# A gated delta rule with two groups of products per chunk, one pass for the weighted keys, and a weight pool at another address

## The chip, the cores and the metric

The kernel runs on one core of one Trainium2 chip. The metric is device time in microseconds (us), the median of several executions; lower is better. PE is the matrix engine (its weight load is listed as PEld), DVE the vector engine, ACT the scalar engine, POOL the GpSimd engine, SP the engine that issues most of the DMAs. Each engine runs its instructions in the order in which they stand in its queue.

## The reference

One decoder layer for 1024 prompt tokens and 8 requests of 4 new tokens each (1056 columns in all), model width 1024, float32:

```
p   = rmsnorm(x) @ w_in          # split: q,k,v of attention | conv input | z | a,b | gate_A | gate_B
o_A = stick-breaking attention   # 8 heads of 64, causal, no softmax
o_B = gated delta rule           # 4 heads, a 128x128 state each
m   = sigmoid(gate_A)*(o_A @ w_pa) + sigmoid(gate_B)*(o_B @ w_pb);   x = x + m @ w_o
x   = x + relu(rmsnorm(x) @ w_up)**2 @ w_down;   y = rmsnorm(x)
```

The part that the change touches is the delta rule, evaluated in chunks of tokens. For each chunk, with the state s of the head, U and W from a triangular solve, and decay factors in the operands:

```
v_new = U-part - W @ s
o     = (q * decay) @ s + (q @ k.T * decay) @ v_new
s     = s * exp(g_last) + (k * decay).T @ v_new
```

## The kernel before

**Number format.** A dense product in float32 is made of three products in the reduced format fp32r: a high part of the weights by a high part of the input (line 140), high weights by low input (141), low weights by high input (142). They are called stream matmuls here: 128x128 weights, and 256, 272 or 288 columns that move past them. The columns are cut into four pieces (`CX`: 256, 256, 256, 288) in the first half of the program and into two halves further on. All other products (of the delta rule, the transposes by `tr`) are plain float32; a 128x128 one stands as "x2" in the profile, that is as two instructions.

**Order.** The whole program is written in Python, but a planner that runs when the program is built decides in which order each engine's queue takes the instructions, from costs of its own; `tc.issue_after` and `tc.high_priority` steer it. In the first half, the dense products (`pd_uq`, `pd_uk`, `pd_uv`: conv inputs of a head; `pd_z`; `pd_aq`, `pd_ak`, `pd_av`: attention's q, k, v; `pd_g`: the gates) fill the queue of PE, and the short products of the delta rule stand between them in small runs. Later parts: attention among the gates' products (from about 600 us), the merge (`pb`, `pa`), output projection (`px`), up projection (`pu`), down projection (`pw`, then `pv`).

**The delta rule.** `gdn_head(h)` is called for the four heads. It solves the triangular systems of all eight chunks of 128 tokens together (U and nw, the negative of W), where line 544 weights the keys of one chunk into the tile kb (two buffers) and line 545 multiplies it by U. Then a loop over the chunks c carries the state st:

- product y (PSUM tile p6): `U.vb` (line 554) plus `nw.st` (line 556);
- DVE scales it into y2 (line 558), ACT copies it into yv (line 560);
- product s (p8): `kn.y2` (line 562), which DVE adds to the decayed state: the next st (line 565);
- product o (p7): `AT.yv` (line 569) plus `qe.st` (line 571), which ACT copies out (572) and squares (573).

p6, p7 and p8 all come from one pool `psg` of two PSUM banks, so the third tile waits for the first to be read. In the profile's names AT is `E`, qe is `cgb`, st is `st`, kn is `kn`. In the order listings a name such as `y0_5` is the tile y of head 0, chunk 5.

**Addresses.** Tiles lie in SBUF one behind the other, pool behind pool. The staging tiles and the two buffers each of `wh` and `wl` in `wpool` hold the weights of `pd_aq`, `pd_ak`, `pd_av`, `pd_g`, of `pb` and `pa`, and of the first pair of conv inputs. The other weights lie in the pools `gw` (further conv inputs, z) and, later, in pools of their own. In the built program, the byte address of a weight tile within a partition, taken modulo 256, and that of the moving columns are:

| product | weights, before | weights, after | moving columns, before | after |
|---|---|---|---|---|
| pd_aq, pd_ak, pd_av, pd_g, first conv pair | 192 | 64 | 0 | 0 |
| pb | 192 | 64 | 128 | 0 |
| pa | 192 | 64 | 0 to 192 | 0 to 192 |
| pd_uk, pd_uq, pd_uv (the rest), pd_z | 64 | 64 | 0 | 0 |
| pu, px | 64 | 64 | 0, second half 128 in places | the same |
| pw | 192 | 192 | 128 | 128 |

The conv job, the z job and the pools further on are laid out so that sizes below them decide their addresses: `z_job` has a tile of T + 48 words, of which T are used.

Of the kernel before, what the change touches and what calls it, by code (L numbers as in the profile page):

```python
# [18 lines left out]
P = 128  # L19
# [19 lines left out]
def hybrid_step(ctx, tc, x_prompt, x_sample, cache_k, cache_v, page_table, state_conv, state_ssm,  # L39
# [13 lines left out]
    cst = pool("cst")  # L53
    wctx = ExitStack()
    wpool = pool("wpool", 2, stack=wctx)
    kctx = ExitStack()
    keep = pool("keep", stack=kctx)
    dr = ctx.enter_context(tc.tile_pool(name="dr", bufs=1, space=DRAM))
# [13 lines left out]
    def gtile(name):  # L72
        return psg.tile([P, 512], F32, tag="g", name=name)
# [30 lines left out]
            w0s.append(st)  # L104
    ident = cst.tile([P, P], F32, name="ident")
    make_identity(nc, ident)
    ones = cst.tile([P, P], F32, name="ones")
    V.memset(ones, 1.0)
    powc = cst.tile([P, 2], F32, name="powc")
# [256 lines left out]
        return (1536 + i * P, f"u{name}", evac), cv  # L366

    def z_job(h):
        z = zp.tile([P, T + 48], F32, tag="zz", name=f"z{h}")[:, 0:T]

        def evac(c, o, n, pt):
            S_.activation(z[:, o:o + n], pt[:, :n], AF.Copy)
            if c == 3:
                S_.activation(z, z, AF.Silu)
                G.tensor_copy(zs[:, h, :], z[:, NP:T])
                SY.dma_start(z_d[h], z[:, 0:NP])

        return 3072 + h * P, f"z{h}", evac
# [10 lines left out]
    def c8(ap):  # L389
        return ap.rearrange("p (c f) -> p c f", f=P)  # L390

    def gdn_head(h):
# [145 lines left out]
        for hf in range(2):  # L538
            hs = slice(hf * 512, (hf + 1) * 512)
            p5 = gtile(f"wt{h}_{hf}")  # L540
            for i in range(4):
                c = hf * 4 + i
                kb = gk.tile([P, P], F32, tag="kb", name=f"kb{h}_{c}", bufs=2)
                V.tensor_scalar(kb, kn[:, cs_[c]], s3[:, c:c + 1], None, op0=ALU.mult)
                PE.matmul(p5[:, i * P:(i + 1) * P], lhsT=kb, rhs=U[:, cs_[c]], start=True, stop=True)
            S_.activation(nw[:, hs], p5, AF.Copy, scale=-1.0)

        on = nw
# [2 lines left out]
        for c in range(NC):  # L551
            sl = slice(c * P, (c + 1) * P)
            p6 = gtile(f"y{h}_{c}")
            PE.matmul(p6[:, 0:P], lhsT=U[:, sl], rhs=vb[:, sl], start=True, stop=(c == 0))
            if c > 0:
                PE.matmul(p6[:, 0:P], lhsT=nw[:, sl], rhs=st, start=False, stop=True)
            y2 = gk.tile([P, P], F32, tag="y2", name=f"y2{h}_{c}", bufs=2)
            V.tensor_scalar(y2, p6[:, 0:P], egc[:, c, h:h + 1], None, op0=ALU.mult)
            yv = gk.tile([P, P], F32, tag="yv", name=f"yv{h}_{c}", bufs=2)
            S_.activation(yv, p6[:, 0:P], AF.Copy)  # L560
            p8 = gtile(f"s{h}_{c}")
            PE.matmul(p8[:, 0:P], lhsT=kn[:, sl], rhs=y2, start=True, stop=True)
            sn = gk.tile([P, P], F32, tag="st", name=f"st{h}_{c}", bufs=2)
            if c > 0:
                V.scalar_tensor_tensor(sn, st, egl[:, c, h:h + 1], p8[:, 0:P], op0=ALU.mult, op1=ALU.add)
            else:
                V.tensor_copy(sn, p8[:, 0:P])
            p7 = gtile(f"o{h}_{c}")
            PE.matmul(p7[:, 0:P], lhsT=AT[:, sl], rhs=yv, start=True, stop=(c == 0))
            if c > 0:  # L570
                PE.matmul(p7[:, 0:P], lhsT=qe[:, sl], rhs=st, start=False, stop=True)
            S_.activation(on[:, sl], p7[:, 0:P], AF.Copy)
            S_.activation(jk_, p7[:, 0:P], AF.Square, accum_out=f_[:, c:c + 1])
            st = sn
# [560 lines left out]
    tbs = [tbp.tile([P, T], F32, name=f"tb{j}") for j in range(KT)]  # L1135
    obctx = ExitStack()
    obp = pool("obp", stack=obctx)
    obh, obl = [None] * 4, [None] * 4

    def ob_tiles(c):  # L1140
# [586 lines left out]
```

## Time and profile before

| | |
|---|---|
| median of three runs | 1692.62 us (1691.89 to 1697.1) |
| profiled execution | 1702.95 us, span 1701.2 us, granted clock 0.994 |
| PE busy in the span | 1656.6 us (97%), 14046 instructions |
| DVE, ACT, POOL busy | 1174.4 us (69%), 778.3 us (46%), 229.7 us (14%) |

The profiled execution took 10.33 us (0.6%) longer than the median of the runs; its span is 1.75 us shorter than its own time. The rows of the groups of instructions give a line of the kernel, an engine, an operation, what it writes and reads, the tile sizes, how many there were, their busy time and the mean duration of one, and the idle time of that engine just before them. A matmul's duration in them (some 280 ns) runs from its start to its end in a pipeline, so the next one starts well before: what PE's time is made of is the distance from start to start, which the timeline shows (columns: start in us, duration in us, engine, line, operation).

### The profile page before, as it was taken

Reading aid. Unit: us, or ns where it says so; the run is one execution under the profiler, and the core shown is the slowest. Engines: PE = TensorE matmul, PEld = TensorE weight load, DVE = VectorE, ACT = ScalarE, POOL = GpSimd, SP = SyncE. Lnnn points to the kernel's source line nnn. Section 1 sums busy time; section 2 is a strip of 40 time slices with the busy share of each in tenths; the row PEclk is TensorE's granted clock in tenths of the full one; section 3 lists DMA queues with packets and bytes.
Section 4 is the critical chain, followed back from the end, with each engine's and each line's share of the span. In section 5 each row is a group of like instructions: output and inputs, shape, how many; then the busy total and the mean of one; then the engine's idle time right before and its main releaser. Section 6 shows DMA issues by size and latency. Waiting matters only on the chain.

```text
span 1701.2 us, 34901 instructions
## 1 busy us (share of the span) xinstructions
PE 1656.6 (97%) x14046; PEld 1603.9 (94%) x14046; DVE 1174.4 (69%) x2363; ACT 778.3 (46%) x1556; POOL 229.7 (14%) x249
## 2 busy tenths in 40 slices
PE   7999999999999999999999999999999999999998
PEld 6999999999998789988999999999999999999998
DVE  6666676877334327889776488887777688688964
ACT  5453434343424225555533356554445563444455
POOL 2120111110004226665300000000000000000000
PEclk9999999999999999999999999999999999999999
DMA  5142233235537567996144645455443665442232
GB/s 182 38 119 81 69 95 106 86 112 147 153 99 216 156 176 168 217 239 190 26 146 131 177 134 146 148 149 172 152 150 115 233 224 208 158 159 97 96 113 78
DMA packets 260207, 240.88 MB, mean 142 GB/s; under 512 B 55907, under 2 KB 217796, under 8 KB 260045
## 3 DMA queue, kind: packets, MB, share of 16 engines
q1 hardware_dynamic: 255094, 227.90, 44.6%
q0 software_dynamic: 3200, 10.52, 2.1%
q8 instruction: 110, 1.80, 0.5%
q10 hardware_dynamic: 1750, 0.23, 0.1%
q14 instruction: 53, 0.43, 0.1%
HBM read 164.02 MB, written 74.58 MB: 140 GB/s over the span
## 4 chain that ended last, share of the span: by engine, by line
PE 86%; DVE 7%; DMA 4%; issue 2%; ACT 1%; SPq 0%; DVEq 0%; POOLq 0%; ACTq 0%
PE pu L142 6%; PE pu L141 6%; PE pu L140 6%; PE pw L142 5%; PE pw L140 5%; PE pw L141 5%; PE pd_g L140 4%; PE pd_g L142 4%; PE pd_g L141 4%; PE wt L114 2%; PE po L1009 1%; PE px L141 1%; PE px L140 1%; PE px L142 1%; PE pa L141 1%
## 5 line engine op out<-in xcount | busy, mean ns | idle before, releaser
L141 PE MATMUL pu<-Xl,uh 128*128 128x272 f32 (+1 forms) x812 | 230.4, 284 | 0.0
L142 PE MATMUL pu<-Xh,ul 128*128 128x272 f32 (+1 forms) x812 | 229.3, 284 | 0.5 <-DVE ul L1272 0.5
L140 PE MATMUL pu<-Xh,uh 128*128 128x272 f32 (+1 forms) x812 | 229.5, 283 | 0.0
L140 PE MATMUL pw<-hc,w 128*128 128x272 f32 (+1 forms) x784 | 219.4, 284 | 2.4 <-ACT w L1536 2.4
L141 PE MATMUL pw<-hc,w 128*128 128x272 f32 (+1 forms) x784 | 219.4, 284 | 0.0
L142 PE MATMUL pw<-hc,w 128*128 128x272 f32 (+1 forms) x784 | 212.6, 284 | 1.5 <-DVE w L1537 1.5
L142 PEld LDWEIGHTS pu<-Xh,ul 128*128 128x128 f32 x812 | 152.8, 189 | 0.7 <-DVE ul L1272 0.7
L140 PEld LDWEIGHTS pu<-Xh,uh 128*128 128x128 f32 x812 | 152.8, 188 | 0.1
L141 PEld LDWEIGHTS pu<-Xl,uh 128*128 128x128 f32 x812 | 152.7, 188 | 0.0
L140 PEld LDWEIGHTS pw<-hc,w 128*128 128x128 f32 x784 | 148.1, 189 | 2.8 <-ACT w L1536 2.6
L140 PE MATMUL pd_g<-xh,wh_g 128*128 128x256 f32 (+1 forms) x512 | 149.7, 292 | 1.1 <-issue 1.1
L142 PE MATMUL pd_g<-xh,wl_g 128*128 128x256 f32 (+1 forms) x512 | 148.9, 291 | 1.2 <-issue 1.2
L141 PE MATMUL pd_g<-xl,wh_g 128*128 128x256 f32 (+1 forms) x512 | 149.2, 291 | 0.0
L141 PEld LDWEIGHTS pw<-hc,w 128*128 128x128 f32 x784 | 147.2, 188 | 0.0
L142 PEld LDWEIGHTS pw<-hc,w 128*128 128x128 f32 x784 | 144.3, 189 | 1.9 <-DVE w L1537 1.9
L140 PEld LDWEIGHTS pd_g<-xh,wh_g 128*128 128x128 f32 x512 | 97.7, 191 | 4.8 <-issue 4.3
L971 DVE TENSOR_TENSOR_SCAN pr<-am 128x127 f32<-128x127 f32 (+7 forms) x64 | 89.8, 1404 | 15.5 <-POOL am L967 11.7
L141 PEld LDWEIGHTS pd_g<-xl,wh_g 128*128 128x128 f32 x512 | 97.7, 191 | 2.9 <-issue 2.6
L142 PEld LDWEIGHTS pd_g<-xh,wl_g 128*128 128x128 f32 x512 | 97.6, 191 | 2.9 <-issue 2.7
L1536 ACT ACTIVATE w<-a 128x512 fp32r<-128x512 f32 x84 | 46.7, 620 | 97.3 <-PE pw L142 87.3
L1509 ACT ACTIVATE hc<-hc 128x528 fp32r<-128x528 f32 x98 | 62.0, 643 | 28.9 <-DMA hc<-hc_d 27.2
L967 POOL TENSOR_SCALAR am<-s 128x128 f32<-128x128 f32 (+7 forms) x64 | 71.8, 1122 | 11.0 <-DVE pr L971 5.8
(588 smaller groups left out, 5058.1 us busy)
## 6 DMA issues: line engine op xcount, KB each, us to landing
hc<-hc_d SPq DMA_DIRECT2D x94, 264.0 KB
hc_d<-t SPq DMA_DIRECT2D x14, 952.0 KB
a<-in_w_down_dram SPq DMA_DIRECT2D x52, 256.0 KB
hc_d<-t SPq DMA_DIRECT2D x13, 896.0 KB
ws_c<-in_w_in_dram SPq DMA_DIRECT2D x16, 512.0 KB
ws_wo<-in_w_o_dram SPq DMA_DIRECT2D x32, 256.0 KB
ua<-in_w_up_dram SPq DMA_DIRECT2D x16, 512.0 KB
ub<-in_w_up_dram SPq DMA_DIRECT2D x16, 512.0 KB
```

The source lines that it names most:

```text
L114: return PE.transpose(out, in_, ident[:k, :k])
L140: PE.matmul(pt[:, :n], lhsT=wh[k], rhs=xh[k], start=(k == 0), stop=False)
L141: PE.matmul(pt[:, :n], lhsT=wh[k], rhs=xl[k], start=False, stop=False)
L142: PE.matmul(pt[:, :n], lhsT=wl[k], rhs=xh[k], start=False, stop=(k == nk - 1))
L967: G.tensor_scalar(am[:, :n], s[:, :n], -1.0, 1.0, op0=ALU.mult, op1=ALU.add)
L971: V.tensor_tensor_scan(pr[:, n - 1:0:-1], am_r, am_r, 1.0, op0=ALU.mult, op1=ALU.bypass)
L1009: PE.matmul(po[64 * r:64 * r + 64, 0:P], lhsT=vn[:, b, rs], rhs=wts[hh, 2 * m + r][:, b * P:(b + 1) * P], start=(b == 0), stop=(b == 2 * m ...
L1509: S_.activation(tl[:, 0], tl[:, 1].bitcast(F32), AF.Copy)
L1536: S_.activation(tl[:, 0], src, AF.Copy)
```

## The change

Three things are done.

1. In `gdn_head`, the tile of o is taken before y2, and `qe.st` follows right behind `nw.st`; `AT.yv` then follows when yv is there, and `kn.y2` is put right behind `AT.yv`. Per chunk there are two groups of float32 products on PE instead of three.
2. The weighted keys of four chunks are made by one DVE instruction (128x512, a multiplication by a broadcast) into a tile `x2` with one buffer, where there were four (128x128) into `kb` with two buffers.
3. A tile `wpad` of 32 words stands first in `wpool`, and the z tile is shorter by 32 words: `wpool`'s weights move by 128 bytes, and what lies behind both stays. A tile `obpad` of 32 words stands first in `obp`, before the tiles obh and obl that move past the weights of `pb`.

```diff
--- before.py
+++ after.py
@@ -53,6 +53,7 @@
     cst = pool("cst")
     wctx = ExitStack()
     wpool = pool("wpool", 2, stack=wctx)
+    wpad = wpool.tile([P, 32], F32, name="wpad", bufs=1)
     kctx = ExitStack()
     keep = pool("keep", stack=kctx)
     dr = ctx.enter_context(tc.tile_pool(name="dr", bufs=1, space=DRAM))
@@ -104,6 +105,7 @@
             w0s.append(st)
     ident = cst.tile([P, P], F32, name="ident")
     make_identity(nc, ident)
+    V.memset(wpad, 0.0)
     ones = cst.tile([P, P], F32, name="ones")
     V.memset(ones, 1.0)
     powc = cst.tile([P, 2], F32, name="powc")
@@ -366,7 +368,7 @@
         return (1536 + i * P, f"u{name}", evac), cv
 
     def z_job(h):
-        z = zp.tile([P, T + 48], F32, tag="zz", name=f"z{h}")[:, 0:T]
+        z = zp.tile([P, T + 16], F32, tag="zz", name=f"z{h}")[:, 0:T]
 
         def evac(c, o, n, pt):
             S_.activation(z[:, o:o + n], pt[:, :n], AF.Copy)
@@ -538,11 +540,10 @@
         for hf in range(2):
             hs = slice(hf * 512, (hf + 1) * 512)
             p5 = gtile(f"wt{h}_{hf}")
+            kb = gk.tile([P, 4, P], F32, tag="x2", name=f"kb{h}_{hf}")
+            V.tensor_tensor(kb, c8(kn[:, hs]), s3[:, hf * 4:hf * 4 + 4].unsqueeze(2).to_broadcast([P, 4, P]), op=ALU.mult)
             for i in range(4):
-                c = hf * 4 + i
-                kb = gk.tile([P, P], F32, tag="kb", name=f"kb{h}_{c}", bufs=2)
-                V.tensor_scalar(kb, kn[:, cs_[c]], s3[:, c:c + 1], None, op0=ALU.mult)
-                PE.matmul(p5[:, i * P:(i + 1) * P], lhsT=kb, rhs=U[:, cs_[c]], start=True, stop=True)
+                PE.matmul(p5[:, i * P:(i + 1) * P], lhsT=kb[:, i], rhs=U[:, cs_[hf * 4 + i]], start=True, stop=True)
             S_.activation(nw[:, hs], p5, AF.Copy, scale=-1.0)
 
         on = nw
@@ -552,23 +553,24 @@
             sl = slice(c * P, (c + 1) * P)
             p6 = gtile(f"y{h}_{c}")
             PE.matmul(p6[:, 0:P], lhsT=U[:, sl], rhs=vb[:, sl], start=True, stop=(c == 0))
+            p7 = gtile(f"o{h}_{c}")
             if c > 0:
-                PE.matmul(p6[:, 0:P], lhsT=nw[:, sl], rhs=st, start=False, stop=True)
+                mark = PE.matmul(p6[:, 0:P], lhsT=nw[:, sl], rhs=st, start=False, stop=True)
+                with tc.issue_after(mark.ins):
+                    PE.matmul(p7[:, 0:P], lhsT=qe[:, sl], rhs=st, start=True, stop=False)
             y2 = gk.tile([P, P], F32, tag="y2", name=f"y2{h}_{c}", bufs=2)
             V.tensor_scalar(y2, p6[:, 0:P], egc[:, c, h:h + 1], None, op0=ALU.mult)
             yv = gk.tile([P, P], F32, tag="yv", name=f"yv{h}_{c}", bufs=2)
             S_.activation(yv, p6[:, 0:P], AF.Copy)
+            mark = PE.matmul(p7[:, 0:P], lhsT=AT[:, sl], rhs=yv, start=(c == 0), stop=True)
             p8 = gtile(f"s{h}_{c}")
-            PE.matmul(p8[:, 0:P], lhsT=kn[:, sl], rhs=y2, start=True, stop=True)
+            with tc.issue_after(mark.ins):
+                PE.matmul(p8[:, 0:P], lhsT=kn[:, sl], rhs=y2, start=True, stop=True)
             sn = gk.tile([P, P], F32, tag="st", name=f"st{h}_{c}", bufs=2)
             if c > 0:
                 V.scalar_tensor_tensor(sn, st, egl[:, c, h:h + 1], p8[:, 0:P], op0=ALU.mult, op1=ALU.add)
             else:
                 V.tensor_copy(sn, p8[:, 0:P])
-            p7 = gtile(f"o{h}_{c}")
-            PE.matmul(p7[:, 0:P], lhsT=AT[:, sl], rhs=yv, start=True, stop=(c == 0))
-            if c > 0:
-                PE.matmul(p7[:, 0:P], lhsT=qe[:, sl], rhs=st, start=False, stop=True)
             S_.activation(on[:, sl], p7[:, 0:P], AF.Copy)
             S_.activation(jk_, p7[:, 0:P], AF.Square, accum_out=f_[:, c:c + 1])
             st = sn
@@ -1135,6 +1137,7 @@
     tbs = [tbp.tile([P, T], F32, name=f"tb{j}") for j in range(KT)]
     obctx = ExitStack()
     obp = pool("obp", stack=obctx)
+    V.memset(obp.tile([P, 32], F32, name="obpad"), 0.0)
     obh, obl = [None] * 4, [None] * 4
 
     def ob_tiles(c):
```

The counts of matmuls, POOL and SP instructions stay the same; DVE has 22 fewer (24 kb products less, two memsets more), ACT has two loads of its function table more. On PE, the passages from a stream matmul into a group of float32 products or transposes fall from 336 to 295 in the built order, as other products stand in the same groups already. From the merge on (pb and everything behind it) PE's order is the same as before.

PE's queue around the products s and o of head 0, chunk 4, before: the delta rule's products stand between stream matmuls of `pd_uv2` and `pd_av0`.

```order
L141 MATMUL pd_av0_2_5016<-xl2_170,wh_av0_4960 128x256
L562 MATMUL s0_4_1387<-y20_4_1383,kn0_1013 128x128
L142 MATMUL pd_av0_2_5016<-xh2_169,wl_av0_4961 128x256
L569 MATMUL o0_4_1391<-yv0_4_1385,E20_1036 128x128
L571 MATMUL o0_4_1391<-st0_3_1373,cgb0_1217 128x128
L140 MATMUL pd_av0_3_5042<-xh3_167,wh_av0_4960 128x288
L141 MATMUL pd_av0_3_5042<-xl3_168,wh_av0_4960 128x288
```

The product s stood alone and o in a group of its own one stream matmul later. PE's queue after the change, head 0, chunk 5, first the group of y and of the first half of o, with a transpose of attention's values (`t8_nv0`) ahead of it:

```order
L116 MATMUL t8_nv0_1_5029<-ident_120,vf0_4911 128x128 x4
L555 MATMUL y0_5_1386<-vb0_1206,U0_1223 128x128
L558 MATMUL y0_5_1386<-st0_4_1382,nw0_1225 128x128
L560 MATMUL o0_5_1388<-st0_4_1382,cgb0_1219 128x128
L142 MATMUL pd_aq1_0_5046<-xh0_175,wh_aq1_5042 128x256
L143 MATMUL pd_aq1_0_5046<-xl0_176,wh_aq1_5042 128x256
```

The product of `cgb` (qe) by the state now stands behind that of nw by the state. Then, 27 rows further on, the group that ends the chunk:

```order
L144 MATMUL pd_aq1_0_5046<-xh0_175,wl_aq1_5043 128x256
L142 MATMUL pd_aq1_1_5073<-xh1_173,wh_aq1_5042 128x256
L565 MATMUL o0_5_1388<-yv0_5_1393,E20_1038 128x128
L568 MATMUL s0_5_1396<-y20_5_1391,kn0_1015 128x128
L143 MATMUL pd_aq1_1_5073<-xl1_174,wh_aq1_5042 128x256
L144 MATMUL pd_aq1_1_5073<-xh1_173,wl_aq1_5043 128x256
```

The product of the state, s, moved from ahead of o to behind its last part.

PE's queue at the step from chunk 0 to chunk 1 of head 2 (`t8_nk` are transposes of attention's keys, `kk3` products of head 3), before:

```order
L140 MATMUL pd_ak2_3_5672<-xh3_167,wh_ak2_5587 128x288
L452 MATMUL kk3_4_3927<-cvk3_3383 128x128
L554 MATMUL y2_1_3240<-vb2_3112,U2_3129 128x128
L556 MATMUL y2_1_3240<-st2_0_3234,nw2_3131 128x128
L453 MATMUL kk3_4_3927<-cvq3_3386,cvk3_3383 128x128
L452 MATMUL kk3_4_3927<-cvk3_3383 128x128
L453 MATMUL kk3_4_3927<-cvq3_3386,cvk3_3383 128x128
```

and after:

```order
L116 MATMUL t8_nk2_0_5655<-ident_120,kf2_5537 128x128 x4
L565 MATMUL o2_0_3194<-yv2_0_3197,E22_2922 128x128
L568 MATMUL s2_0_3200<-y22_0_3195,kn2_2899 128x128
L555 MATMUL y2_1_3206<-vb2_3090,U2_3107 128x128
L558 MATMUL y2_1_3206<-st2_0_3202,nw2_3109 128x128
L116 MATMUL t8_nk2_1_5660<-ident_120,kf2_5537 128x128 x4
L560 MATMUL o2_1_3208<-st2_0_3202,cgb2_3103 128x128
L142 MATMUL pd_av2_0_5678<-xh0_175,wh_av2_5674 128x256
```

The products y of chunk 1 stand now directly behind s of chunk 0, from which their state comes, where stream matmuls lay between them before.

PE's queue at the first scores of attention (`sc0_0`, `sc0_1`: head 0's first blocks; `pd_g1_4_0` is piece 0 of the fifth column tile of gate B), before:

```order
L142 MATMUL pd_g1_4_0_7502<-xh0_173,wl_g1_4_7497 128x256
L114 MATMUL dwt1_6451<-ident_119,ds1_6439 128x128 x2
L114 MATMUL dwt1_6451<-ident_119,wx1_6448 32x128
L961 MATMUL sc0_0_0_7722<-kh0_6268,qs0_6267 128x128
L962 MATMUL sc0_0_0_7722<-kl0_6269,qs0_6267 128x128
L961 MATMUL sc0_1_0_7733<-kh0_6268,qs0_6267 128x256
L962 MATMUL sc0_1_0_7733<-kl0_6269,qs0_6267 128x256
L140 MATMUL pd_g1_4_1_7528<-xh1_171,wh_g1_4_7496 128x256
```

and after:

```order
L143 MATMUL pd_g0_5_3_7646<-xl3_170,wh_g0_5_7562 128x288
L144 MATMUL pd_g0_5_3_7646<-xh3_169,wl_g0_5_7563 128x288
L963 MATMUL sc0_0_0_7676<-kh0_6222,qs0_6221 128x128
L964 MATMUL sc0_0_0_7676<-kl0_6223,qs0_6221 128x128
L963 MATMUL sc0_1_0_7687<-kh0_6222,qs0_6221 128x256
L964 MATMUL sc0_1_0_7687<-kl0_6223,qs0_6221 128x256
L142 MATMUL pd_g1_5_0_7765<-xh0_175,wh_g1_5_7759 128x256
```

The first scores stand later, behind 7 more pieces of the gates' products of 24 stream matmuls each; attention's last scores stand at the same piece (`pd_g1_7_3`) in both.

## The prediction

> **What bounds the kernel.** I read the page's engine totals first, then its chain of work that ended last, then the windows, and last the timeline of PE.
>
> ```profile
> PE 1656.6 (97%) x14046; PEld 1603.9 (94%) x14046; DVE 1174.4 (69%) x2363; ACT 778.3 (46%) x1556; POOL 229.7 (14%) x249
> PE 86%; DVE 7%; DMA 4%; issue 2%; ACT 1%; SPq 0%; DVEq 0%; POOLq 0%; ACTq 0%
> ```
>
> PE is busy 97% of the span of 1701.2 us; only 1701.2 - 1656.6 = 44.6 us are left for every wait, the start and the end included. So a change can gain in two ways only: it takes work off PE, or it makes PE's work run denser. Nothing is taken off here (the matmuls are the same in number), so what counts is the distance from one matmul's start to the next. The timeline of PE shows two values for the same shape, here first and last of 20 and of 28 matmuls in a row:
>
> ```profile
> 76.73 0.28 PE L141 MATMUL pd_z<-xl,wh_z 128*128 128x256 f32 x1
> ...
> 78.89 0.28 PE L142 MATMUL pd_z<-xh,wl_z 128*128 128x256 f32 x1
> 147.77 0.28 PE L140 MATMUL pd_z<-xh,wh_z 128*128 128x256 f32 x1
> ...
> 150.95 0.28 PE L140 MATMUL pd_z<-xh,wh_z 128*128 128x256 f32 x1
> ```
>
> (78.89 - 76.73)/19 = 0.1137 us in the first stretch, (150.95 - 147.77)/27 = 0.1178 us in the second: two paces, about 4 to 5 ns apart, of one product. Which of them runs can also be read from the mean duration, in groups by shape of two short windows (the first is 548 to 555 us, the second 145 to 153 us):
>
> ```profile
> L140 PE MATMUL pd_g<-xh,wh_g 128*128 128x256 f32 x18 | 5.0, 276 | 0.0
> L140 PE MATMUL pd_z<-xh,wh_z 128*128 128x256 f32 x23 | 6.5, 281 | 0.0
> ```
>
> 276 ns is the fast pace, 281 the slow one. Over the whole run, the groups by shape of 256 columns are:
>
> ```profile
> L140 PE MATMUL pd_g<-xh,wh_g 128*128 128x256 f32 x384 | 111.0, 289 | 0.0
> L140 PE MATMUL pd_aq<-xh,wh_aq 128*128 128x256 f32 x96 | 27.9, 290 | 1.4 <-DVE ql L822 1.2 <-DVE vsT L826 0.2
> L140 PE MATMUL pd_ak<-xh,wh_ak 128*128 128x256 f32 x96 | 27.3, 284 | 0.0
> L140 PE MATMUL pd_av<-xh,wh_av 128*128 128x256 f32 x96 | 27.6, 288 | 0.0
> L140 PE MATMUL pb<-obh,wh_pb 128*128 128x256 f32 x96 | 28.9, 301 | 1.3 <-DVE tb L1177 1.1 <-ACT obh L1158 0.2
> L140 PE MATMUL pw<-hc,w 128*128 128x256 f32 x392 | 109.8, 281 | 2.4 <-ACT w L1536 2.4
> L140 PE MATMUL pu<-Xh,uh 128*128 128x256 f32 x364 | 101.3, 279 | 0.0
> L140 PE MATMUL px<-mh,wh_wo 128*128 128x256 f32 x128 | 35.4, 278 | 0.0
> ```
>
> The last three stand in pure stretches of stream matmuls. Those with weights 64 past a multiple of 256 bytes (pu, px) take 278 to 279 ns on average, about half fast; those with weights at 192 (pw) take 281, all slow. The rows above them are mixed with float32 groups, which lengthen the matmul beside them, so their means can't be set against the paces.
>
> **The weight pool's address.** The change moves the weights of `wpool` from 192 to 64. The 256-column matmuls that read them are 384 of pd_g, 96 each of pd_aq, pd_ak and pd_av, for each of three lines, 3 x 672 = 2016, and about 144 of the first conv pair (counted in the built program): 2160. What is gained by one isn't shown by a trace in which the same tile stands at both addresses. Nearest are the rows of pw and of pu and px: 281 - 279 = 2 ns. That times 2160 gives -4.3 us, and I take it. One bound is 0 (the address has nothing to do with the pace: pd_z at 64 is fast in one stretch and slow in the other, and pd_g at 192 is fast at 548 us, so it isn't the address alone); the other is all slow to all fast, 5 ns x 2160 = -10.8 us. A loss would need matmuls slower than 281, and the 64 class shows none. pb and pa have another 96 x 3 + 64 x 3 = 480 of 256 columns; the pace in them can't be read from their means. I take half of the 2 ns, 480 x 1 = -0.5 us, between 0 and 480 x 5 = -2.4.
>
> **Two groups instead of three.** What a group costs is read where one and two float32 products stand between stream matmuls of 256 and 288 columns:
>
> ```profile
> 217.12 0.28 PE L141 MATMUL pd_av<-xl,wh_av 128*128 128x256 f32 x1
> 217.23 0.39 PE L562 MATMUL s<-y,kn 128*128 128x128 f32 x2
> 217.37 0.36 PE L142 MATMUL pd_av<-xh,wl_av 128*128 128x256 f32 x1
> 217.58 0.38 PE L569 MATMUL o<-yv,E 128*128 128x128 f32 x2
> 217.79 0.39 PE L571 MATMUL o<-st,cgb 128*128 128x128 f32 x2
> 217.94 0.38 PE L140 MATMUL pd_av<-xh,wh_av 128*128 128x288 f32 x1
> 218.16 0.30 PE L141 MATMUL pd_av<-xl,wh_av 128*128 128x288 f32 x1
> ```
>
> From s at 217.23 to o at 217.58 (one product and one stream matmul) 0.35 us; from one product to the next in a group, 217.79 - 217.58 = 0.21; a stream matmul alone is 0.118. So the group costs 0.35 - 0.21 - 0.118 = 0.02 us beyond its contents. The second group checks it: from 217.58 to 218.16 is 0.58 us against 2 x 0.21 + 0.13 = 0.55, which is 0.03. The built order has 336 - 295 = 41 groups fewer: 41 x 0.01 to 0.03, -0.4 to -1.2 us, and I take -0.4, since a start is shown only to a hundredth. The work on PE is the same otherwise, and DVE and ACT do the same for each chunk.
>
> What the new order puts on the chain: `AT.yv` stands ahead of `kn.y2` and needs yv.
>
> ```profile
> L554 PE MATMUL y<-vb,U 128*128 128x128 f32 x64 | 12.6, 278 | 0.3 <-DVE st L565 0.3
> L558 DVE TENSOR_SCALAR y<-y,egc 128x128 f32<-128x128 f32 x32 | 11.6, 362 | 27.1 <-PE y L556 27.1
> L560 ACT ACTIVATE yv<-y 128x128 f32<-128x128 f32 x32 | 8.9, 277 | 33.4 <-DVE y L558 33.4
> 224.11 0.39 PE L562 MATMUL s<-y,kn 128*128 128x128 f32 x2
> 224.60 0.33 DVE L565 SCALAR_TENSOR_TENSOR st<-st,egl,s 128x128 f32<-128x128 f32 x1
> ```
>
> yv begins only when y2 is done (all of ACT's 33.4 us of idleness before it are put down to that DVE line), so the last group of a chunk can begin 0.277 us later, and s, from which the next state comes, 0.21 us after that: 0.5 us per chunk, 32 chunks, 16 us of chain. It costs PE nothing as long as stream matmuls lie between: in the listing of head 0, chunk 5, 27 rows (27 x 0.118 = 3.2 us) against 0.362 + 0.277 = 0.64 us. Where the cover is missing it costs. At head 2, chunk 0, the product y of chunk 1 stands right behind s: it needs the bank of s, which is free when the new state is written. By the last two rows that is 224.60 + 0.33 - 224.11 = 0.82 us after the start of s, of which s's own 0.21 is work: 0.6 us of wait. The new order has three other places with no cover (a transpose and two first matmuls behind the reading of their bank), and the old one has some of its own (the 0.3 us before `U.vb` and 1.2 before pd_aq for `ql` are two); I set the balance to 0, with ends of -3 and +3 us, five waits of 0.6 fewer or more.
>
> **The pass for the weighted keys.** The line of kb and those who wait for it:
>
> ```profile
> L544 DVE TENSOR_SCALAR kb<-kn,s x32: 244/285/1140, 105.6 to 449.0; 128x128 f32<-128x128 f32 x32
>   PEld wt L545: 0.5, 2
>   PE wt L545: 0.2, 1
> L1419 DVE TENSOR_TENSOR us<-ub 128x512 f32<-128x512 f32 x16 | 10.9, 680 | 0.0
> ```
>
> 32 x 0.285 = 9.1 us of DVE become 8 x 0.680 = 5.4 us (priced by the nearest row of that shape and operation): DVE has 3.7 us less, off the path. PE's waits for kb, 0.2 us, can go: -0.2. The first product of a half starts 0.680 - 0.285 = 0.4 us later after kn's scale is there, and the second half's pass must wait for four products of the first, both once per half: covered by the stream matmuls, as the tile's other four products wait for nothing any more; up to 8 x 0.4 = +3 us if never covered. The two more loads of ACT's table:
>
> ```profile
> 178.12 1.28 ACT L442 ACT_TABLE_LOAD   x1
> ```
>
> 2 x 1.28 = 2.6 us on an engine that is busy 46% (778.3 us of the span): 0 on the path.
>
> **Sum.** -4.3 - 0.5 - 0.4 + 0 - 0.2 = -5.4 us. Against the profiled execution, 1702.95 us, that is 1697.5 us (a span of about 1695.8); that execution is 10.3 us longer than the median of the runs, which I leave out as the same on both sides. Against the median, 1692.62 - 5.4 = 1687.2 us. Less than 0.3% (5.1 us, about what a measurement of this kernel can tell from no change) would be more than 1687.5.
>
> **Rival 1: the address does nothing.** For it: both paces occur at both addresses (the rows of pd_z and pd_g above), so the pace may be set by where in PE's rhythm a stretch begins. Against it: pw stands at 281 over 392 matmuls and px at 278 over 128, both in pure stretches of the same shape. Time: 1692.62 - 0.4 - 0.2 = 1692.0. The Trainium skill, "SBUF — State Buffer", section "Who interferes with whom", says that PE never waits for anyone, and "TensorE: Matmul & The Clock Gate", Part 2, that the two read ports of weights and moving columns are independent; by that an address should not matter, and the sum would be this rival's. The two durations, 276 and 281 ns for one shape, show that something does.
>
> **Rival 2: mostly fast.** If the new class runs as px does where its columns lie at 0 as well (276 ns where it is fast), four fifths of 5 ns come: 2160 x 4 = -8.6, with the rest -1.1: 1682.9 us.
>
> **Rival 3, slower: attention starts too late.** Its first scores stand 7 x 24 = 168 stream matmuls later, 168 x 0.118 = 20 us of PE's work, and its end stays. The load on DVE there:
>
> ```profile
> 600.00:700.00 100.00, 98.24 (x813) 90.24 (x810) 55.79 (x59) 43.15 (x95) 43.75 (x47) 0.98 0.72 179
> 700.00:800.00 100.00, 95.79 (x788) 84.50 (x787) 91.97 (x82) 57.28 (x120) 60.98 (x57) 0.98 0.86 223
> 800.00:900.00 100.00, 98.32 (x845) 92.22 (x844) 74.98 (x137) 43.11 (x90) 21.24 (x30) 0.98 0.29 90
> L971 DVE TENSOR_TENSOR_SCAN pr<-am 128x127 f32<-128x127 f32 (+7 forms) x64 | 89.8, 1404 | 15.5 <-POOL am L967 11.7
> ```
>
> Behind the length of each window stand the busy times of PE, PEld, DVE, ACT and POOL. DVE's share between 600 and 700 is 56%: 20 us of that, 11 us, must be done later, and between 700 and 800 DVE has only 8 us idle (91.97 busy), and its scans wait for POOL anyway (15.5 us before L971, 11.7 of them for L967). If nothing of it fits, PE waits for 11 us behind DVE: 1687.2 + 11 = 1698 us. It decides for slower when more than 10.5 us (5.4 + 5.1) are waited for. Against it: from 800 to 900 DVE has 25 us idle, and nowhere in the new order do the blocks stand denser among the gates' pieces than at the densest place of the old one.
>
> **How the numbers follow.** The forecast with 1 to 3 ns per matmul (-2.2 to -6.5, other terms -1.1) has 0.50, and splits at 0.3% into 0.28 faster and 0.22 the same; its own range is 1685 to 1690. Rival 2 has 0.18 (faster), rival 1 0.17 (0.15 the same, 0.02 faster by the other terms), rival 3 0.15 (slower). Faster 0.48, same 0.37, slower 0.15. The bottom of the range is rival 2 with pa and pb at their bound, 1682.9 - 1.9 = 1681; the top is 1697.5, next to rival 3, which is mostly left out.
>
> **What would show it.** The mean of pd_g's 256 columns should fall by about 2 ns from 289, px, pu and pw stay at theirs. In the order of the trace, s should follow o within 0.25 us. L544 (by its new line) should show 8 instructions of about 0.68 us. PE's busy share should stay at 97 to 98%, its idle time near 44.6 us. The forecast is wrong if pd_g stays at 289 (rival 1), falls to 285 (rival 2), or if PE's busy time between 700 and 800 us falls from 95.79 to under 90 (rival 3).

## The result: 1.2% slower, where 0.3% faster was forecast

The changed kernel takes 1715.33 us (median of 6 runs, 1709.67 to 1716.99) against 1693.76 us for the kernel before (6 runs): a ratio of 1.0117, 95% interval 1.0097 to 1.0136, some 20 us slower, and outside the forecast's range of 1681 to 1697.5. Lines of the kernel stand two further down in its rows than before (142 to 144 for the stream matmuls), from the loop on by other amounts.

The page of the changed kernel, the totals and the chain that ended last:

```profile
PE 1656.8 (97%) x14046; PEld 1605.3 (94%) x14046; DVE 1170.6 (68%) x2341; ACT 779.8 (46%) x1558; POOL 223.2 (13%) x249
PE 80%; DVE 7%; DMA 6%; issue 2%; SPq 1%; ACT 1%; POOL 1%; DVEq 0%; POOLq 0%; ACTq 0%
```

PE is busy for as long as before (1656.8 against 1656.6 us), but the span is 1713.8 us, so PE stands idle 57.0 us instead of 44.6, and its share of the chain that ended last falls from 86% to 80%. That isn't all. The granted clock of the profiled executions is 0.994 before and 0.989 after. The clock records in the traces have two values only, 1 and 0.5; the mean says how long the half lasted. Half of a stretch at half clock is lost, 10.8 us before and 19.3 us after, but only where PE has work in it. At the end of the changed kernel, for instance, PE does nothing for 4.4 us at a clock of 0.50 (behind the length: five busy times, then the clock):

```profile
1709.40:1713.80 4.40, 0.00 (x0) 0.00 (x0) 0.00 (x0) 0.00 (x0) 0.00 (x0) 0.50 0.59 217
```

Such stretches are idle time already. Before, 2.3 of the 10.8 us fall on idle time of PE, after, 4.4 of the 19.3. A span is then idle time + clock lost while PE was busy + the work at full clock (added up from the matmul and clock records; as stream matmuls at half clock start 0.21 us apart, not quite twice the 0.12, the lost clock is put about a tenth too high, and the work that much too low):

| profiled execution | span | PE idle | clock lost while busy | work at full clock | measured ratio to before |
|---|---|---|---|---|---|
| before | 1701.2 | 44.6 | 8.5 | 1648.1 | |
| pads alone | 1687.1 | 41.3 | 3.3 | 1642.4 | 0.9984 (0.9970 to 0.9998) |
| two groups and one pass, no pads | 1718.0 | 59.7 | 14.4 | 1643.9 | 1.0115 (1.0093 to 1.0136) |
| all three (the changed kernel) | 1713.8 | 57.0 | 14.9 | 1641.9 | 1.0117 (1.0097 to 1.0136) |

The work got 6.2 us shorter; the forecast had 5.4. That near agreement is partly luck, since the work isn't a property of the instructions alone: the same instructions at the same addresses in another order (yv first, below) have 1648.4 us. Waits and clock took 12.4 + 6.4 = 18.8 us. The execution of before that was profiled was one of its longer ones; the pads alone have its order to the row and an ordinary profile, so they are the cleaner partner. Against them the change has 15.7 us more idle time and 11.5 us more lost clock. Windows of the changed kernel and then of the pads alone (behind the length: busy time of PE, PEld, DVE, ACT, POOL) show where:

```profile
90.00:520.00 430.00, 414.01 (x3669) 406.32 (x3668) 254.67 (x621) 168.05 (x390) 39.47 (x38) 0.98 0.34 101
690.00:900.00 210.00, 198.78 (x1691) 180.94 (x1691) 171.83 (x205) 107.76 (x226) 95.49 (x102) 0.98 0.62 161
```

```profile
90.00:520.00 430.00, 424.73 (x3819) 417.95 (x3818) 274.43 (x704) 171.75 (x408) 45.52 (x45) 1.00 0.37 113
690.00:900.00 210.00, 203.47 (x1724) 186.23 (x1723) 174.59 (x245) 102.78 (x215) 78.97 (x85) 0.99 0.57 156
```

PE is busy 10.7 us less in the delta rule's part (90 to 520 us) and 4.7 less in attention (690 to 900). The waits of PE from 90 to 900 us, by what it waited for (us in total, times, longest), are in the changed kernel:

```profile
PE pb L143 <- DVE obl L1162: 5.2, 1, 5.2
PE l L508 <- DVE U L499: 4.0, 1, 4.0
PE pd_aq L142 <- DVE ql L824: 3.0, 1, 3.0
PE wt L116 <- DVE s L974: 3.0, 2, 2.6
PE t_nv L116 <- ACT ntv L834: 2.0, 2, 1.3
PE y L558 <- DVE st L571: 1.8, 1, 1.8
```

Only the last, 1.8 us, is on the products that were moved. In the others PE waits for DVE's and ACT's other work: the transposed inverse U, the reading of a bank of pd_aq, and obl, the low part of pb's moving columns. The wait for obl isn't new; it is longer than in the pads alone:

```profile
PE pb L143 <- DVE obl L1162: 3.5, 2, 2.8
```

The wait of the moved product isn't harmless either. It stands where the next chunk's y comes soon behind s, while DVE works at the keys of a later head (cvk), and another wait follows it, for ACT:

```profile
308.90 0.49 PE L558 MATMUL y<-st,nw 128*128 128x128 f32 x2 [1.82 <-DVE st L571]
311.46 0.58 PE L142 MATMUL pd_uv<-xh,wh_uv 128*128 128x256 f32 x1 [1.41 <-ACT upv L357]
```

From 309.95 to 316.8 us the clock records show half clock. One of the other waits followed back, in rows of SP, ACT, DVE and PE at head 2 (start, duration):

```profile
350.43 0.40 SPq L591 DMA_DIRECT2D o_d<-zl  x1
353.38 0.34 SPq L494 DMA_DIRECT2D cgb<-cg_d  x1
358.86 1.06 ACT L495 ACTIVATE cgb<-cgb 128x1024 f32<-128x1024 f32 x1 [3.89 <-DMA cgb<-cg_d]
359.95 1.23 DVE L496 TENSOR_TENSOR cgb<-cvq,cgb 128x1024 f32<-128x1024 f32 x1 [5.08 <-ACT cgb L495]
361.10 0.42 DVE L824 TENSOR_TENSOR ql<-pd_aq,qh 128x256 f32<-128x256 f32 x1
361.57 0.58 PE L142 MATMUL pd_aq<-xh,wh_aq 128*128 128x256 f32 x1 [3.04 <-DVE ql L824]
```

zl, the tile in which a head's output is multiplied by z, is stored at the head's end; zl of head 1 and qe of head 2 have the same tile. The store leaves at 350.43 us (342.72 before); qe's load follows 3 us later, ACT waits for it, DVE stands idle for 5.08 us before the multiplication of qe, and behind that, in DVE's queue, stands ql (the low part of attention's q), which frees the bank that PE needs. What comes after PE's wait costs nearly as much again. The same pd_aq, next:

```profile
366.12 0.41 PE L142 MATMUL pd_aq<-xh,wh_aq 128*128 128x256 f32 x1
366.33 0.41 PE L143 MATMUL pd_aq<-xl,wh_aq 128*128 128x256 f32 x1
...
368.02 0.28 PE L142 MATMUL pd_aq<-xh,wh_aq 128*128 128x256 f32 x1
368.14 0.28 PE L143 MATMUL pd_aq<-xl,wh_aq 128*128 128x256 f32 x1
```

Until 368.0 us matmuls start 0.21 us apart, then 0.12: from the wait's end at 361.57, PE ran for 6.4 us at half its clock, of which some 3 us are lost, behind a wait of 3.0. "TensorE: Matmul & The Clock Gate" of the Trainium skill, Part 1, describes such a gate: half the clock after an idle window of about 3.4 us. The trace agrees with the half; the wait that half clock followed here is 3.04 us long, and shorter ones can do it too (last section).

### The profile page after: what moved, and what is told of

Same layout as the page of the kernel before. It is cut to its first block, busy times and chain, and to the rows that moved or that the text cites. A ratio compares the mean times of both kernels' runs of the same rounds, so it can differ in the third digit from the quotient of the medians.

```text
span 1713.8 us, 34882 instructions
## 1 busy us (share of the span) xinstructions
PE 1656.8 (97%) x14046; PEld 1605.3 (94%) x14046; DVE 1170.6 (68%) x2341; ACT 779.8 (46%) x1558; POOL 223.2 (13%) x249
## 4 chain that ended last, share of the span: by engine, by line
PE 80%; DVE 7%; DMA 6%; issue 2%; SPq 1%; ACT 1%; POOL 1%; DVEq 0%; POOLq 0%; ACTq 0%
PE pu L144 6%; PE pu L143 6%; PE pu L142 6%; PE pw L144 5%; PE pw L142 5%; PE pw L143 5%; PE pd_g L143 3%; PE pd_g L142 3%; PE pd_g L144 3%; DMA xr<-in_x_prompt_dram 2%; PE px L143 1%; PE px L144 1%; PE px L142 1%; PE wt L116 1%; PE pv L142 1%
## 5 line engine op out<-in xcount | busy, mean ns | idle before, releaser
L973 DVE TENSOR_TENSOR_SCAN pr<-am 128x127 f32<-128x127 f32 (+7 forms) x64 | 91.5, 1429 | 14.9 <-POOL am L969 11.0
```

The source lines that it names most:

```text
L973: V.tensor_tensor_scan(pr[:, n - 1:0:-1], am_r, am_r, 1.0, op0=ALU.mult, op1=ALU.bypass)
```

## The experiments

**Each part alone.** The pads, the two groups and the pass each by itself on the kernel before, and the two without the pads. The edits are the pieces of the diff.

> The kernel before with the pads alone (wpad, the shorter z tile, obpad); every engine's order is the one of before. If the address sets the share of fast matmuls: the 256-column matmuls of wpool start about 1.5 to 2 ns closer to one another on average, 2160 of them, so 3 to 5 us faster (about 1689 to 1691 us). Rival, the address does nothing: 1692 to 1695 us, and pd_g keeps its mean of 289 ns.

Measured: 1689.02 us, ratio 0.9984 (0.9970 to 0.9998), 3.5 us faster. Of the starts of two neighbouring 256-column matmuls of pd_g, 10% lay under 115.5 ns apart (fast) before and 44% in this run (mean 117.3 and 116.0 ns, counted over all such pairs of the trace that are less than 130 ns apart); pd_av went from 19% to 63%. The group row shows it too (289 ns before):

```profile
L142 PE MATMUL pd_g<-xh,wh_g 128*128 128x256 f32 x384 | 109.9, 286 | 0.0
```

So the products of wpool run faster with the pads, as forecast, in an order that is the same but for two small memsets more on DVE. All the traces of this case bear it out: in the ten without pads 3 to 20% of pd_g's pairs are fast, in the eight with them 39 to 55%; in the first conv pair 0 to 4% and 40 to 78%. But products whose weights and columns stand at the same addresses modulo 256 in both kernels change as well: pd_uv gets slower (59 to 78% fast without the pads, 29 to 43% with them), pd_z by tendency faster (35 to 66%, 45 to 83%). That the pads move the pace is shown; that the address of a product's own weights decides it isn't.

> The kernel before with the two groups per chunk alone. Theory 1, the longer chain of each head frees the buffer shared by qe and zl later, DVE stands idle before qe's multiplication and PE waits for what stands behind it: 10 to 18 us slower (1703 to 1712 us), with the idle time of DVE before the multiplication of qe (ACT's Exp before it) well above the 9.6 us of before. Theory 2, the pass for the weighted keys with its single buffer is to blame: within 3 us of before.

Measured: 1701.77 us, 1.0050 (1.0034 to 1.0067), 9 us slower: in the direction of theory 1, just under its range. DVE waits 13.0 us for ACT's Exp of qe, a little over the 9.6 of before.

> The kernel before with the one pass for the weighted keys of four chunks alone. Theory 1 (the chain of the two groups is to blame): within 3 us of before, since DVE has 3.7 us less to do and the rest is covered. Theory 2 (the pass is to blame): 10 to 18 us slower. Theory 3, any other order of the queues loses what the old order had: both this one and the two groups alone lose 5 us or more.

Measured: 1706.69 us, 1.0086 (1.0067 to 1.0104), 14 us slower. Both lose, and the pass more: theory 1 alone is out, as is theory 2 alone, and theory 3, that both lose 5 us or more, has come true.

> The changed kernel without the pads; its order on every engine is the one of the changed kernel. If the pads gain 3 to 5 us: 1718 to 1720 us. If the pads do nothing, 1715 us; if the address makes the changed kernel slower, under 1713 us.

Measured: 1713.95 us, 1.0115 (1.0093 to 1.0136). With the pads 1.0117: in this order the pads' gain doesn't show in the time, the case that was to be expected if the pads did nothing, though the work at full clock falls by 2.0 us (1643.9 to 1641.9, table above); with medians over runs that scatter by 10 us a gain may be hidden.

**The pass: is it the shared tile?** The weighted keys now lie in x2, one buffer, which sqt, the first step of the next head, uses as well. In the changed kernel DVE waits for it (first row), which before it never did, and for qe (second row; third row: before):

```profile
DVE sqt L412 <- PE wt L546: 10.2, 3, 3.4
DVE cgb L496 <- ACT cgb L495: 23.3, 4, 10.6
```

```profile
DVE cgb L494 <- ACT cgb L493: 9.6, 4, 4.2
```

So the next head's start waits for this head's products. Two edits tell the tile from the pass: the pass in its own tile, and four short passes into the shared one. Of the first edit only the line of the tile is shown; the others move a small tile of the start and let Square write over o in PSUM.

```diff
-            kb = gk.tile([P, 4, P], F32, tag="x2", name=f"kb{h}_{hf}")
+            kb = gk.tile([P, 4, P], F32, tag="kb", name=f"kb{h}_{hf}")
```

> The pass for the weighted keys alone, but in a tile of its own instead of the tile x2, which the next head's first step (sqt, the sums of squares) also uses. To make room, Square's unused output goes to PSUM and a small tile of the start moves. Theory S, the shared tile ties the next head's start to this head's products: about the time of before, 1690 to 1696 us, no wait of DVE's sqt for the products wt, and the triangular inverse U of heads 1 to 3 ready near 244, 343 and 423 us as before. Rival R, any newly planned order loses: 1700 us or more, as in the pass alone (1706.7).

```diff
+            kb = gk.tile([P, 4, P], F32, tag="x2", name=f"kb{h}_{hf}")
             for i in range(4):
...
-                V.tensor_scalar(kb, kn[:, cs_[c]], s3[:, c:c + 1], None, op0=ALU.mult)
+                V.tensor_scalar(kb[:, i], kn[:, cs_[c]], s3[:, c:c + 1], None, op0=ALU.mult)
```

> The kernel before with its four short passes for the weighted keys, but into the shared tile x2 (one buffer) that the changed kernel uses. Theory S: the sharing alone costs what the pass alone cost, 1702 to 1711 us, and U of heads 1 to 3 comes some 17 to 37 us later than before. Rival, it is the long pass of 128x512 on DVE that loses: about 1693 us.

Measured: 1706.2 us, 1.0087 (1.0074 to 1.0100), for the own tile; 1713.02 us, 1.0129 (1.0114 to 1.0144), for the four passes into the shared one. Theory S falls as an account of the time: it had 1690 to 1696 us for the own tile. What it said of the mechanism came. The stores of zl, first and last, of before, of the changed kernel, and of the pass in its own tile:

```profile
L589 SPq DMA_DIRECT2D o_d<-zl x4: 319/323/338, 255.8 to 508.1; - x4
```

```profile
L591 SPq DMA_DIRECT2D o_d<-zl x4: 320/366/1472, 256.3 to 543.5; - x4
```

```profile
L587 SPq DMA_DIRECT2D o_d<-zl x4: 319/335/391, 253.7 to 506.6; - x4
```

The fourth head ends 35 us late in the changed kernel; with the tile apart it ends as early as before (506.6), no wait of sqt is left, and PE's wait for obl is 3.0 us instead of 5.2. The time doesn't come back. Against the pads alone, this run has 3.7 us more of idle time of PE (45.0) and 6.0 more of lost clock (9.3); the rest of its 15.4 us longer span is work at full clock (1648.1), as before without the pads. Two of its waits:

```profile
PE t_nk L114 <- ACT ntk L830: 3.7, 3, 3.3
PE pd_uk L142 <- DVE wl_uk L131: 1.6, 1, 1.6
```

A transpose of attention's keys waits 3.3 us for ACT, in an operation that doesn't use the tile. Which of these waits the new order brought, and which the pass itself, these rows don't tell. And the whole changed kernel with the tile apart:

> The changed kernel with the weighted keys in a tile of their own (as in kb_own_tile). Theory S: what is left is the loss of the two groups and the gain of the pads, 1701.8 - 3.5 = 1698 us, within 3. Rival R: 1708 us or more.

Measured: 1711.25 us, 1.0109 (1.0094 to 1.0123): theory S forecast 1698, rival R 1708 or more.

**The groups: is it the longer chain?** The second group with s first:

```diff
-            mark = PE.matmul(p7[:, 0:P], lhsT=AT[:, sl], rhs=yv, start=(c == 0), stop=True)
             p8 = gtile(f"s{h}_{c}")
+            mark = PE.matmul(p8[:, 0:P], lhsT=kn[:, sl], rhs=y2, start=True, stop=True)
             with tc.issue_after(mark.ins):
-                PE.matmul(p8[:, 0:P], lhsT=kn[:, sl], rhs=y2, start=True, stop=True)
+                PE.matmul(p7[:, 0:P], lhsT=AT[:, sl], rhs=yv, start=(c == 0), stop=True)
```

> The two groups per chunk alone, but with the state's product kn.y2 ahead of AT.yv in the second group. Theory C, the longer chain from state to state (0.28 us of yv and 0.21 us of AT.yv, 8 chunks, 4 heads, so some 16 us in all) is what the groups cost: half or more of the 9 us come back, 1693 to 1698 us, and head 3's last state comes 8 us or more earlier than in the two groups alone. Rival, the newly planned order itself costs it: 1700 to 1704 us.

Measured: 1699.31 us, 1.0040 (1.0024 to 1.0056), against 1.0050 with o first; the intervals overlap. The last store of zl leaves at 520.9 us instead of 524.8, so half of the 8 us came. Undecided between the two, and small either way.

**Orders without the change.** If what costs is that the planner orders the queues anew, an edit that changes nothing must cost as well. Three edits on the kernel before were meant for this; only the first leaves the chain from state to state and the tiles between the heads as they were:

```diff
-            S_.activation(on[:, sl], p7[:, 0:P], AF.Copy)
             S_.activation(jk_, p7[:, 0:P], AF.Square, accum_out=f_[:, c:c + 1])
+            S_.activation(on[:, sl], p7[:, 0:P], AF.Copy)
```

> The kernel before with two lines of the chunk loop exchanged: ACT squares o first and copies it out after. The same instructions, none on the chain from state to state; but the planner now gives the queues another order from head 0 on. Theory R, a newly planned order loses what the old one happens to have (few waits of PE between 90 and 900 us): 1697 to 1708 us, with PE idle more than the 15 us that before has there and a lower granted clock. Rival, the loss comes from what the change does: 1691 to 1695 us.

```diff
-            V.tensor_scalar(y2, p6[:, 0:P], egc[:, c, h:h + 1], None, op0=ALU.mult)
...
             S_.activation(yv, p6[:, 0:P], AF.Copy)
+            V.tensor_scalar(y2, p6[:, 0:P], egc[:, c, h:h + 1], None, op0=ALU.mult)
```

> The kernel before with the lines of y2 and yv exchanged: ACT copies y before DVE scales it. The same instructions; kn.y2 comes up to 0.28 us later per chunk. Theory R: 1697 to 1708 us. Rival, only what the change does counts: 1692 to 1696 us (32 x 0.28 us of chain are covered by stream matmuls).

```diff
+            S_.activation(rs_[:, 0:1], p7[:, 0:1], AF.Copy)
             S_.activation(jk_, p7[:, 0:P], AF.Square, accum_out=f_[:, c:c + 1])
```

> The kernel before with one more ACT instruction per chunk, a copy of one column of o (32 of some 0.2 us, 6 us on an engine that is busy 46%). Theory R: 1697 to 1712 us. Rival: 1692 to 1696 us.

Measured, on a chip where before took 1699.99 us, 6 us more than on the first, so that the ratios count and not the expected times: 1704.54 us, 1.0036 (1.0020 to 1.0052), for Square first; 1709.91 us, 1.0054 (1.0034 to 1.0074), for yv first; and 1785.7 us, 1.0500 (1.0481 to 1.0519), for the one-column copies. The first, with the same instructions as before, costs hardly less than the two groups; its fourth head ends at 511.6 us, 3.5 us later than before. One sign of theory R failed: its granted clock is 0.996, not lower than the 0.994 of before. The second lengthens the chain too, as y2 now waits for yv: its fourth head ends at 520.2 us. The third costs 86 us, outside both theories' ranges, and it isn't an edit that changes nothing: it writes in every chunk into rs_, a tile with one buffer, into which the next head sums its squares. So the next head's start waits for the last copy of this head, and the sums of the fourth head come 170 us later (the first row is before, the others this run, with DVE's waits for the copy):

```profile
L412 DVE TENSOR_REDUCE rs<-sqt x16: 666/682/686, 67.6 to 366.4; 128x16 f32<-128x512 f32 x16
```

```profile
L412 DVE TENSOR_REDUCE rs<-sqt x16: 666/685/686, 68.2 to 536.1; 128x16 f32<-128x512 f32 x16
  ACT rs L573: 1.8, 3
```

Its fourth head ends at 630.2 us, 122 us late. Its waits of PE:

```profile
PE dkt L114 <- DMA kg<-in_cache_k_dram,idx: 10.4, 2, 9.7
PE dwt L114 <- DVE ds L912: 7.9, 1, 7.9
PE pb L141 <- DVE obl L1160: 5.5, 1, 5.5
```

PE is idle 100.3 us in that run and loses 32.8 us to the clock while busy (the granted clock is 0.973); its work at full clock is 1649.7 us, near that of before: what it lost are waits and clock. How much of that comes from the tie between the heads and how much from the new order isn't separated. For the other two the parts can't be compared: before wasn't profiled on this chip; Square first has 46.1 us idle, 5.1 lost to the clock and 1651.6 of work at full clock.

**The change in other orders.** The instructions of the changed kernel in four more orders, on a chip where before took 1700.56 us: the two exchanges of lines above, s first as above, and zl in a buffer of E1:

```diff
-        zl = gk.tile([P, NP], F32, tag="cgb", name=f"zl{h}")
+        zl = gk.tile([P, NP], F32, tag="E1", name=f"zl{h}", bufs=2)
```

> The changed kernel with the two ACT lines on o exchanged (Square first, then the copy): the same instructions in another planned order. If the order is what costs: the ratio to before lies anywhere from 0.995 to 1.02, off the changed kernel's 1.0117 by more than 0.003. If the operations cost it: 1.009 to 1.014.

> The changed kernel with the lines of y2 and yv exchanged, so that yv, which the second group needs first, comes first: the same instructions in another planned order. Order: a ratio off 1.0117 by more than 0.003. Operations: 1.009 to 1.014.

> The changed kernel with kn.y2 ahead of AT.yv in the second group. Order: a ratio off 1.0117 by more than 0.003. The longer chain from state to state: some 5 us less than the changed kernel, about 1.008. Operations otherwise: 1.009 to 1.014.

> The changed kernel with zl in a buffer of E1 instead of the tile that qe uses, so that qe's load doesn't wait for the store of the head before; another planned order from the start on. If the 23 us for which DVE stands idle before qe's multiplication are what PE waits for between 300 and 460 us: that idle time falls under 10 us and the ratio to 1.003 or less. Order: the ratio is off 1.0117 by more than 0.003 in either direction while DVE's idle time there falls all the same.

Measured: 1.0104 (1.0074 to 1.0134), 1.0070 (1.0046 to 1.0094), 1.0093 (1.0064 to 1.0122) and 1.0124 (1.0089 to 1.0159). Only yv first leaves the changed kernel's 1.0117 by more than 0.003, the sign that was set for the order. The other three lie within 0.003 of it, where the expectations had put the operations, and none comes near before. The wait for qe, the one followed back above, isn't the cause either: with zl apart DVE's wait for it falls as expected, and PE waits elsewhere (first row DVE, then PE):

```profile
DVE cgb L496 <- ACT cgb L495: 8.3, 4, 4.1
```

```profile
PE wt L116 <- DVE s L974: 6.4, 1, 6.4
PE pb L142 <- DVE tb L1180: 5.4, 2, 2.7
```

**More pads.** With the weights of the down projection at 64 and its columns at 0:

```diff
     h2 = pool("h2", 12, stack=fctx)
+    pad(h2, 32, "h2gap")
```

> The pads alone plus 128 bytes in front of the tiles hc of the down projection: its weights go from 192 to 64 and its moving columns from 128 to 0 (modulo 256). The order of PE, DVE, ACT and SP is the one of the pads alone (POOL has one memset more). If the address sets the share of fast matmuls: pw's 1176 matmuls of 256 columns start some 2 to 3 ns closer, 2.5 to 3.5 us less than the pads alone, 1685.5 to 1686.5 us, and pw's mean falls from 281 to about 279 ns. If not: 1689 us and 281 ns.

Measured: 0.9979 (0.9969 to 0.9990), no different from the pads alone (0.9984), and pw didn't move:

```profile
L142 PE MATMUL pw<-hc,w 128*128 128x256 f32 x392 | 109.7, 281 | 2.4 <-ACT w L1540 2.4
```

The pads move the pace of wpool's products, but "weights at 64, columns at 0" isn't the rule for it: pw now has both, and 2% of its pairs are fast, as before. No kernel that was run is measurably faster than the kernel before with the pads alone.

## Why the prediction was wrong, point by point

- **The step that failed: the balance of waits, set to 0 with ends of -3 and +3.** It measured 12.4 us against the profiled execution of before and 15.7 against the pads alone. I weighed the tight spots that I could see on PE's own queue, beside the moved products. Most of the new waits stand on DVE's and ACT's queues, whose order the planner had changed as well, and reach PE through operations that the diff doesn't touch. What I failed to price was that all queues had been planned anew from head 0 on, against an order with less than 6 us of waits in 430 us of delta rule. That the step failed is measured; why these waits arose is followed through for a few of them only.
- **A term that was missing: the granted clock.** It cost 6.4 us (11.5 against the pads alone), half as much as the waits or more. I left the clock out because before showed 0.994; but before's losses also stand behind its waits, so a wait of PE has to be priced at up to twice its length. Not every wait costs that: behind 2.4 us at 1347 us, before, the clock stays at 1.00.
- **The cover of the longer chain.** Nearly true for the single chunk: PE's wait for a state's update is 1.8 us in all, at one place, where 0.6 was priced for one at which the cover is missing; the half clock behind it wasn't priced. False for the head: the chain's end moved from 508.1 to 543.5 us, and what hangs on it (the tile of zl and qe, attention's start) moved with it. The shared tile had the larger part: the pass alone ends at 541.6 us, with a tile of its own at 506.6, the two groups alone at 524.8. But an early end alone doesn't bring the time back (1.0087 with the tile apart).
- **The pass: "covered by the stream matmuls".** Its duration was right (8 of 681 ns, forecast 680; no one waited for it). I priced its wait for the first half's products and overlooked that x2 is also the tile of the next head's sqt, with 10.2 us of waits of DVE.

```profile
L544 DVE TENSOR_TENSOR kb<-kn,s x8: 677/681/693, 178.7 to 479.0; 128x512 f32<-128x512 f32 x8
```

- **The pads: -4.3 - 0.5.** Right in sign and size, in the old order: 3.5 us in time (interval 0.3 to 5.1), 5.7 in work at full clock. The 2 ns per matmul measured 1.3 for pd_g (117.3 to 116.0) and 1.9 for pd_av (117.0 to 115.1). In the changed kernel pd_g's row, which I had named as the sign, shows 288 ns instead of 289, as its mean also holds matmuls at half clock; from start to start the pace came (45% of the pairs fast). Rival 1, the address does nothing, is contradicted by the pads alone, and so is what I drew for it from the Trainium skill ("SBUF — State Buffer", section "Who interferes with whom"), that an address should not matter; whether PE waits at a port no run here shows. My own reason, the class of the address, is contradicted by pw and by pd_uv. The size was partly luck.
- **Fewer groups: -0.4.** Not contradicted: the work at full clock is 1.3 us shorter with the two groups alone (1648.1 to 1646.8), which is less than the orders differ by among themselves.
- **Rival 3** had the sign and one of the places: PE waits 5.2 us for obl in attention, which begins later (3.5 us in the pads alone). It had 0.15, the price of one place; the delta rule's part lost more than twice as much. The sign that I named for it, under 90 us of busy PE between 700 and 800, wasn't reached (91.28).

What stays open: how the 20 us divide between the order and the operations. One order that was planned anew without any new dependence cost 0.4%; another, with a longer chain, 0.5%. The change in six orders with all its parts (the tile apart among them) costs 0.7 to 1.2%. So one newly planned order by itself cost about a third of what the change costs. That the operations themselves bring waits that no order avoids isn't shown and isn't excluded, as there is no run of the change in the old order.

## What to carry to other kernels

Where a planner sets the queues and PE is 97% busy, price an edit by what its new plan does on every engine's queue, and run a null edit first: here one that only exchanged two lines cost 0.4%. A null edit must not lengthen a chain or write into a one-buffer tile of the next head: 32 one-column copies that did so cost 5%. Edits that left the queues' order as it was (here the pads) came within a few microseconds of the forecast; those that replanned didn't. A new user of a shared one-buffer tile ties two heads together, and one wait of PE of 3 us cost about twice its length here.

## What the hardware showed unexpectedly

- After PE's wait of 3.04 us the matmuls ran 0.21 us apart for 6.4 us, then 0.12 again; after one of 4.04 us (459.42 us) they did so until 463.4. The lost clock of a run goes with its waits: 3.3 us with 41.3 us of idle time, 32.8 with 100.3. But the length of one wait doesn't decide: before, the clock falls to 0.71 (605 to 610 us) behind waits of 0.75 and 0.40 us, and stays at 1.00 behind one of 2.4 (1347 us).
- The pace of one shape moves between two values, 113 and 118 ns from start to start, and 128 bytes shift how often each occurs (pd_g: 10% to 44% fast) in the same order; pd_uv, which wasn't moved, changed the other way (78% to 43%), and for pw the same shift did nothing (281 ns). What sets the pace wasn't found.
